# Three more block-product pairs in place of six dense gates, with the page scores moved beside the attention heads

## The chip, the cores and the metric

The kernel runs on one core of a Trainium2 chip. Five engines with queues of their own do the work: PE (TensorE, matrix products, with its weight loads shown as PEld), DVE (VectorE), ACT (ScalarE), POOL (GpSimd) and SP (SyncE, which here only issues transfers). POOL issues transfers too, and all gathers. The metric is the device time of one execution in microseconds (us); lower is better. Cited line numbers, such as L220, are lines of the kernel before.

## The reference

One step of one decoder layer, in float32, for a prompt of 512 tokens and 8 further sequences with one new token each. The kernel puts both side by side as 520 columns (`N`). Cut to what matters:

```python
h = modulate(rmsnorm(x, norm1_w), sh1, sc1)      # shift/scale from a conditioning product with w_ada
mq, mk, mv, mo, mi, mf, fq, fk, fv, ff, ga, gb = split(h @ w_in + b_in)
y_m = mlstm(mq, mk, mv, mo, mi, mf)              # 4 heads, matrix memory
q_f, k_f = rmsnorm(fq, f_qnorm_w), rmsnorm(fk, f_knorm_w)   # per head, 8 heads of 128
y_f = fox(q_f, k_f, fv, log_sigmoid(ff))         # attention with forgetting; the 8 new tokens
                                                 # also attend to 2 pages of 128 cached keys each
merged = sigmoid(ga) * (y_m @ w_proj_a) + sigmoid(gb) * (y_f @ w_proj_b)
x = x + g1 * (merged @ w_out)
h2 = modulate(rmsnorm(x, norm2_w), sh2, sc2)
x = x + g2 * conv_ffn(h2)                        # width 2 x 5632, causal convolution of width 3
```

`ga` and `gb` are 2048 wide: 16 chunks of 128 rows each. The code calls them first gates (0 to 15) and second gates (16 to 31).

## The kernel before

**Precision and tiling.** Everything is stored feature-major: 128 features on the partitions, 520 tokens along the row. A float32 product is made from three products of rounded parts: weights and inputs are split into a high part (a cast on ACT) and a low part (a subtraction on DVE), and high x high, high x low and low x high are added up. The 520 tokens are two halves of 260 columns.

**Dense chunks.** `dense` (L211) makes one chunk of 128 output rows. For 2048 inputs it has 16 steps of six products, 96 products in all. Weights come 8 steps at a time: `wraw` (L162) loads 512 KB on the SP queue into one of eight `raw` tiles, `wtwo` splits them (ACT cast at L177, DVE subtraction at L178) into two pairs of `wh`/`wl` buffers. After each step one entry of the list `bg` is run, which is how the attention work of an earlier head gets in between the products. Before each 8 steps `due` (L189) may run one step of `pending`: an eighth of a conditioning product (`ada_steps`, L504), which takes four `raw` tiles.

**Pairs.** `Pair` (L260) makes two chunks together. The 2 x 2 blocks (two output chunks by two halves of the inputs, against two halves of the tokens) are combined before and after, so that seven block products do for eight: seven times 24 products of 260 columns, 168 in all. `run_pairs` drives a list of pairs with every DVE, ACT and PE instruction in program order. `GatePair` (L1023) applies the sigmoid and writes to DRAM (`dmg` for first gates, `dsg` for second gates).

**Stages around the change**, in order: the mLSTM heads with two first gates done densely (`NG` is 2: gates are made until `bg` is empty); 16 chunks of `y_m @ w_proj_a`; twelve pairs (first gates 2 to 15 and second gates 0 and 1, with the four pairs of attention values); the attention heads, 16 dense chunks `f_proj` (L1254), a query and a key chunk for each of 8 heads; the second gates 2 to 15, 14 dense chunks `w_gate`; 16 chunks of `y_f @ w_proj_b` (8 steps each); then `w_out`, the feed-forward part and the end.

**Attention work in `bg`.** For each head: `f_norm_q`, `f_norm_k` (each with a reciprocal root by `rsqrt`, L360), `f_forget`, `f_values`, four `f_scores`, four `f_turn`, four `f_attend`, at fixed slots of the chunks that follow. A slot is one step of a dense chunk.

**Page work.** The 8 new tokens attend to gathered pages, in steps that all start after the last head: `s_rows` turns the queries into rows and writes them to DRAM; sixteen times `s_load` (queries broadcast by SP, two gathers of keys by POOL) and `s_scores` (on DVE, two multiplications of 512 columns and two reductions); `s_bias`, `s_softmax`, `s_weights`; 32 `s_gather` of values, eight `s_attend` and four `s_heads`. They lie in the 224 slots of the 14 gates.

**What sets the order.** Outside the pairs a planner fixes each engine's order in advance from its own costs. Weight loads and splits are given the highest priority, the rest goes by the order of the text. Tiles of one tag are handed out in the order of the text, each waiting for a free buffer. On the chip each queue then runs in that order, so a waiting instruction holds all behind it.

Of the kernel before, what the change touches and what calls it, by code (L numbers as in the profile page):

```python
# [63 lines left out]
def tile_hybrid_step(ctx: ExitStack, tc: tile.TileContext, I, O):  # L64
# [116 lines left out]
    def wsplit(src, raw=None):  # L181
        with tc.high_priority():
            return wtwo([raw or wraw(src)], src.shape[1])

    pending = []
    calls = [0, 1, 1]
    bg, slow = [], []
# [171 lines left out]
    def rsqrt(parts, scale, out=None):  # L359

        v, r, t = pt("rv"), out or st("rr"), pt("rt")
        for ps, a, b in parts:
            S.activation(r[:, a:b], ps, AF.Ln, scale=scale, bias=eps)
            V.tensor_scalar(v[:, a:b], ps, scale, EPS, op0=ALU.mult, op1=ALU.add)
        o = slice(parts[0][1], parts[-1][2])
        S.activation(r[:, o], r[:, o], AF.Exp, scale=-0.5)
        V.tensor_tensor(t[:, o], r[:, o], r[:, o], op=ALU.mult)
# [132 lines left out]
    def ada_steps(which):  # L500

        box = []
        col0 = which * DM

        def part(k):
            if k == 0:
                box.append(mm_ps("adp"))
            raw = [[wraw(I["w_ada"][i * P:(i + 1) * P, col0 + e * 1024:col0 + (e + 1) * 1024]) for e in range(2)]
                   for i in (k, k + 1)]
            for i in (k, k + 1):  # L510
                ada_mm(box[0], [(i, raw[i - k][g // 2][:, g % 2 * 512:(g % 2 + 1) * 512], i == 0, i == KC - 1)
                                for g in range(4)], False)
# [448 lines left out]
        for i, (a, b) in enumerate(((w[0], x[0]), (w[0], x[1]), (w[1], x[0]))):  # L961
            T.matmul(ps, a, b, start=(first and i == 0), stop=(last and i == 2))

    def on(f, *a):
        return lambda: f(*a)

    for hh in range(MH):
        H = Head()
        H.i, H.vt, H.hm, H.v, H.o = hh, [], [], [], []
# [48 lines left out]
                G.dma_start(dxf[i + 8 * (n == 4)][:, :N], t[:, :N])  # L1018


    dsg = dram([NG, P, N], "dsg")

    class GatePair(Pair):  # L1023
        def __init__(self, gates, order):
# [75 lines left out]
                self.out(0)  # L1100
                self.__dict__.clear()

    gates = list(range(NG, KC + NG))
    units = [GatePair(gates[2 * i:2 * i + 2], ORDER if i else ORDER1) for i in range(KC // 2)]
    units[2:2] = [ValuePair((2 * i, 2 * i + 1)) for i in range(FH // 2)]


# [58 lines left out]

    qwc = mconst([P, 1], "qwc")
    V.tensor_scalar(qwc, col(C_QN), DK ** -0.5, None, op0=ALU.mult)
    qS = mconst([P, NS, FH], "qS")
    kS = mconst([P, NS, FH], "kS")  # L1170
    vS = mconst([P, NS, FH], "vS")
    yf = []

# [4 lines left out]
    def f_norm_k(H):  # L1178
        f_norm(H.k, col(C_KN), H)
        G.dma_start(O["kT"][:, H.i, :], H.k[:, :N])  # L1180
        V.tensor_copy(kS[:, :, H.i], H.k[:, SEQ:N])
        H.kr = split(sp, "s", H.k, "fk", SEQ, G)

    def f_norm_q(H):
        if H.i == 0:
            log_exp()
        f_norm(H.q, qwc, H)
        V.tensor_copy(qS[:, :, H.i], H.q[:, SEQ:N])
        H.qr = split(sp, "s", H.q, "fq", SEQ, G)

    def f_square(H, t):
# [38 lines left out]
    def f_turn(H, j):  # L1230

        w = SEQ - j * P
        ps = mm_ps("fPT")
        for i in range(j, NB):
            T.transpose(ps[:, (i - j) * P:(i - j + 1) * P], H.p[i][:, j * P:(j + 1) * P], ident)
        if j == NB - 1:
            S.copy(H.last[:, P:2 * P], ps[:, :P])
            H.p = None
        else:
            H.pt.append(split(sp, "s", ps, "fp", w))  # L1240

    def f_attend(H, j):
        if j == 0:
            H.y = mm_ps("fy")
        o = slice(j * P, (j + 1) * P)
        if j < NB - 1:
            three(H.y[:, j * P:], [t[:, o] for t in H.vt], [t[:, :SEQ - j * P] for t in H.pt[j]], j == 0, False)
            H.pt[j] = None
# [14 lines left out]
    def slots(at):  # L1263
        bg.extend(at.get(i) for i in range(KC))

    heads = []
    for hh in range(FH + 1):
        if hh < FH:
            H = Head()
            H.i, H.p, H.pt = hh, [], []  # L1270
            H.v = st("fi")
            nc.sync.dma_start(H.v[:, :N], dv[hh])
            heads.append(H)
        A = heads[hh - 1] if hh > 0 else None
        first_half, second_half = {}, {}
        if A:
            first_half = {4: on(f_norm_k, A), 6: on(f_forget, A), 8: on(f_values, A),
                          14: on(f_scores, A, 0), 15: on(f_scores, A, 1)}
            second_half = {0: on(f_scores, A, 2), 2: on(f_scores, A, 3)}
            second_half.update({7 + j: on(f_turn, A, j) for j in range(NB)})  # L1280
            second_half.update({12 + j: on(f_attend, A, j) for j in range(NB)})
        if hh < FH:
            second_half[5] = on(f_norm_q, H)
        slots(first_half)
        if hh == FH:
            bg.extend(second_half.get(i) for i in range(KC))
            break
        H.q = f_proj(H, 0)
        f_square(H, H.q)
        slots(second_half)  # L1290
        H.k = f_proj(H, 1)
        f_square(H, H.k)


    dqf = dram([NS, FH * P], "dqf")
    sc = mconst([P, NPG, NS, FH], "sc")
    pp = st("pp")
    yS = mconst([P, NS, FH], "yS")

    def s_rows():  # L1300
        ps = mm_ps("qSt")
        T.transpose(ps[:64, :P], qS.rearrange("p b h -> p (b h)"), ident)
        qrow = pt("qrow")
        V.tensor_copy(qrow[:64, :P], ps[:64, :P])
        nc.sync.dma_start(dqf.rearrange("b (h d) -> (b h) d", h=FH), qrow[:64, :P])

    def s_load(i):

        b, e = divmod(i, 2)
        qb = pt("qb")  # L1310
        nc.sync.dma_start(qb[:, :512], dqf[b, e * 512:(e + 1) * 512].partition_broadcast(P))
        W.k[i] = [qb]
        for g in range(NPG):
            kp = pt("kp")
            gather(kp[:, :512], I["cache_k"], idx_h[e][:, b * NPG + g:b * NPG + g + 1])
            W.k[i].append(kp)

    def s_scores(i):
        b, e = divmod(i, 2)
        qb, *kps = W.k.pop(i)  # L1320
        v = Ordered(tc, nc.vector)
        for g, kp in enumerate(kps):
            v.tensor_tensor(kp[:, :512], kp[:, :512], qb[:, :512], op=ALU.mult)
            v.tensor_reduce(sc[:, g, b, e * 4:e * 4 + 4], kp[:, :512].rearrange("p (h d) -> p h d", h=4),
                            axis=AX.X, op=ALU.add)

    def s_bias():
        V.tensor_tensor(sc, sc, sbias, op=ALU.add)

    def s_softmax():  # L1330
        pqk = pt("pqk")[:, :64]
        V.tensor_tensor(pqk, qS.rearrange("p b h -> p (b h)"), kS.rearrange("p b h -> p (b h)"), op=ALU.mult)
# [24 lines left out]
    def s_gather(i):  # L1357

        e, g, b = i // 8 % 2, i // 4 % 2, i // 16 * 4 + i % 4
        W.v[i] = pt("vp")  # L1360
        gather(W.v[i][:, :512], I["cache_v"], idx_h[e][:, b * NPG + g:b * NPG + g + 1])

    def s_attend(n):
# [23 lines left out]
    bg += [s_rows] + [None] * 12 + [on(s_load, 0), None, None, on(s_load, 1)] + [None] * 5  # L1387
    for i in range(NS * 2):
        bg += [on(s_scores, i), None] + ([on(s_load, i + 2)] if i + 2 < NS * 2 else []) + [None] * 2
    bg += [s_bias, None, s_softmax] + [None] * 6 + [s_weights] + [None] * 4  # L1390
    bg += [on(s_gather, i) for i in range(6)] + [None] * 4
    for n in range(8):
        bg += [on(s_attend, n)] + [on(s_gather, i) for i in range(n * 4 + 6, min(n * 4 + 10, 32))]
        bg += [on(s_heads, n // 2)] if n % 2 else [None]
        bg += [None] * 3
    mg = []
    for j in range(KC):
        if j == 0:
            assert not pending
            pending += ada_steps(SH2)  # L1400
            calls[:] = 0, 1, 4
        if j < NG:
            mg.append(st("sgm"))
            nc.sync.dma_start(mg[j][:, :N], dsg[j])
        else:
            mg.append(w_gate(j, 1))
    flush()
    for hh in range(FH):
        hi, lo = yf[hh]
        S.copy(hi[:, SEQ:N], yS[:, :, hh])  # L1410
# [144 lines left out]
    for n, j in enumerate(order):  # L1555
# [642 lines left out]
```

## Time and profile before

| | us |
|---|---|
| median of 3 runs | 2924.07 |
| lowest, highest | 2920.72, 2925.45 |
| profiled execution | 2922.52 |
| its span | 2920.8 |
| PE busy in it | 2859.3 |

The profile is of one execution. "Busy" is the time in which at least one instruction of an engine ran. A group of instructions stands with its line, engine and operation, what it writes and reads, its count and the mean of one. Matmuls overlap, so that the mean of one (about 283 ns) is longer than the step from one to the next. The chain of waits says which engine waited for which; the windows give busy times of a stretch of the span.

The stages named above lie at these times of the span: pairs 564 to 809 us, attention heads 809 to 1063, second gates 1063 to 1265, `w_proj_b` 1265 to 1359.

### The profile page before, as it was taken

How to read it: one execution, taken by the hardware profiler on the slowest of the kernel's cores; microseconds unless marked ns; L12 is line 12 of the kernel's file. 1: busy time of each engine (PE TensorE's matmuls, PEld its weight loads, DVE VectorE, ACT ScalarE, POOL GpSimd, SP SyncE). 2: the span in 40 equal slices, each digit the busy share in tenths (PEclk: the TensorE clock that was granted, in tenths of full speed). 3: DMA queues.
4: the chain of work that ended last, by engine and by line, in shares of the span. 5: the costliest groups of instructions: out<-in, count | busy, mean ns of one | idle time of the engine just before them, and what ended most of it. 6: DMA issues, size and time to landing. Idle time of an engine off the chain costs nothing. (4 is left out here: it accounts for less than half of the span.)

```text
span 2920.8 us, 58505 instructions
## 1 busy us (share of the span) xinstructions
PE 2859.3 (98%) x23531; PEld 2737.8 (94%) x23531; DVE 2172.4 (74%) x3950; ACT 1311.3 (45%) x2244; POOL 433.0 (15%) x686
## 2 busy tenths in 40 slices
PE   6999999999999999999999999999999999999999
PEld 4889998999999898899999999999999999999999
DVE  4777875577856657258888888888888888787787
ACT  3234433355544442234555544444444445544543
POOL 0003430211111124311121000000000001100100
PEclk9999999999999999999999999999999999999999
DMA  9933448845444458766772344444434436746742
GB/s 339 302 115 111 151 124 271 292 149 167 157 163 141 139 184 292 261 212 210 216 244 83 113 145 142 134 140 143 151 126 149 137 127 178 196 157 189 201 161 87
DMA packets 211640, 510.92 MB, mean 175 GB/s; under 512 B 23136, under 2 KB 75728, under 8 KB 211368
## 3 DMA queue, kind: packets, MB, share of 16 engines
q1 hardware_dynamic: 175152, 414.37, 43.9%
q0 software_dynamic: 35776, 92.58, 10.7%
q8 instruction: 184, 3.01, 0.4%
q14 instruction: 88, 0.72, 0.1%
q10 hardware_dynamic: 440, 0.23, 0.0%
HBM read 438.77 MB, written 64.86 MB: 172 GB/s over the span
## 5 line engine op out<-in xcount | busy, mean ns | idle before, releaser
L60 PE MATMUL x<-bf,wh 128*128 128x260 f32 x2624 | 477.4, 283 | 1.0 <-DVE tg L60 0.5
L60 ACT CAST wh<-sw 128x512 fp32r<-128x512 f32 x616 | 353.1, 621 | 246.1 <-PE z L60 87.1
L60 DVE TENSOR_TENSOR wl<-sw,wh 128x512 fp32r<-128x512 f32 x616 | 396.5, 685 | 77.1 <-ACT wh L60 73.9
L60 DVE TENSOR_TENSOR wl<-raw,wh 128x1024 fp32r<-128x1024 f32 (+2 forms) x307 | 326.1, 1072 | 118.2 <-ACT wh L60 111.3
L60 PEld LDWEIGHTS x<-bf,wh 128*128 128x128 f32 x2624 | 403.6, 188 | 1.4 <-DVE tg L60 0.7
L60 ACT CAST wh<-raw 128x1024 fp32r<-128x1024 f32 (+2 forms) x307 | 281.8, 929 | 252.9 <-PE x L60 128.7
L60 PE MATMUL x<-bf,wl 128*128 128x260 f32 x1312 | 369.7, 282 | 0.0
L178 DVE TENSOR_TENSOR wl<-raw,wh 128x1024 fp32r<-128x1024 f32 (+1 forms) x152 | 185.5, 1221 | 202.4 <-ACT wh L177 201.9
L177 ACT CAST wh<-raw 128x1024 fp32r<-128x1024 f32 (+1 forms) x152 | 156.8, 1032 | 357.3 <-PE gate L220 114.2
L60 PEld LDWEIGHTS x<-bf,wl 128*128 128x128 f32 x1312 | 247.1, 188 | 0.0
L60 PE MATMUL y<-bf,wh 128*128 128x260 f32 x1312 | 238.5, 282 | 2.8 <-ACT wh L60 2.3
L60 PEld LDWEIGHTS y<-bf,wh 128*128 128x128 f32 x1312 | 201.1, 188 | 3.2 <-ACT wh L60 2.5
L60 DVE TENSOR_TENSOR sw<-raw,raw 128x512 f32<-128x512 f32 x304 | 195.3, 683 | 0.8 <-DMA tot<-sq 0.8
L60 PE MATMUL x<-ff,wh 128*128 128x260 f32 x1024 | 186.0, 282 | 0.0
L60 PE MATMUL y<-bf,wl 128*128 128x260 f32 x656 | 184.6, 281 | 0.2 <-DVE wl L60 0.2
L60 PEld LDWEIGHTS x<-ff,wh 128*128 128x128 f32 x1024 | 157.7, 188 | 0.0
L60 PE MATMUL x<-ff,wl 128*128 128x260 f32 x512 | 144.6, 282 | 0.0
L60 PE MATMUL fo<-fe,wh 128*128 128x260 f32 x768 | 125.5, 284 | 1.1 <-DVE fo L60 0.9
L60 PEld LDWEIGHTS y<-bf,wl 128*128 128x128 f32 x656 | 123.3, 188 | 0.4 <-DVE wl L60 0.4
L60 PE MATMUL z<-bf,wh 128*128 128x260 f32 x656 | 121.3, 285 | 0.0
L60 PEld LDWEIGHTS z<-bf,wh 128*128 128x128 f32 x656 | 100.7, 188 | 13.4 <-issue 13.4
L220 PE MATMUL fi<-hh,wh 128*128 128x260 f32 x512 | 108.9, 294 | 0.0
(589 smaller groups left out, 7624.7 us busy)
## 6 DMA issues: line engine op xcount, KB each, us to landing
raw<-in_w_fi SPq DMA_DIRECT2D x176, 512.0 KB, 4.2
raw<-in_w_in SPq DMA_DIRECT2D x156, 512.0 KB, 4.8
ar<-in_w_ada SPq DMA_DIRECT2D x192, 256.0 KB, 5.9
raw<-in_w_ada SPq DMA_DIRECT2D x96, 512.0 KB, 4.2
raw<-in_w_fo SPq DMA_DIRECT2D x64, 512.0 KB, 4.1
raw<-in_w_out SPq DMA_DIRECT2D x32, 512.0 KB, 5.3
raw<-in_w_fo SPq DMA_DIRECT2D x32, 384.0 KB, 3.9
dff<-cc POOLq DMA_DIRECT2D x44, 260.0 KB, 4.2
```

The lines of the kernel that those rows point to most:

```text
L60: return lambda *a, **k: self.tc.keep_in_program_order(getattr(self.eng, op)(*a, **k))
L177: S.copy(wh[:, o], t[:, :m])
L178: V.tensor_tensor(wl[:, o], t[:, :m], wh[:, o].bitcast(F32), op=ALU.subtract)
L220: T.matmul(acc[:, z, :HN], a[:, o], b[:, z * HN:(z + 1) * HN], start=(k == 0 and i == 0), stop=(k == K - 1 and i == 2))
```

## The change

- Second gates 2 to 7 are made in three more pairs; `GatePair` now does 22 gates. Eight second gates (8 to 15) stay dense. Gates 0 to 7 are fetched from `dsg` during the `w_proj_b` stage, two chunks ahead (`fetch_gate`).
- The bookkeeping of slots becomes a dictionary `plan` from slot to steps, filled by `at(chunk, slot, step)`, with chunks 0 to 15 the heads and 16 to 23 the eight gates.
- The page scores are split by heads: heads 0 to 3 have their `s_rows` at chunk 7 and their eight loads and scores in chunks 8 to 15, beside the later heads; heads 4 to 7 have them in chunks 16 to 18, five slots apart. Values are gathered from chunk 18 on, eight ahead of the first use, half of them into another tile tag.
- The two gathers of one load go into one `raw` tile (the tag of the weight tiles) instead of two small ones, and one multiplication and one reduction of 1024 columns replace two of 512.
- `rsqrt`: the copy of scaled variance plus eps (two halves) and the square move from DVE to ACT.
- `f_turn` does the last block together with the second one; two `f_scores` share a slot.
- Conditioning steps: the last step of a product is now an entry of its own in `pending`; both products of this part are queued at once and run one in three calls in the heads, one in four in the gates, one in two in `w_proj_b`.

```diff
@@ rsqrt
         for ps, a, b in parts:
             S.activation(r[:, a:b], ps, AF.Ln, scale=scale, bias=eps)
-            V.tensor_scalar(v[:, a:b], ps, scale, EPS, op0=ALU.mult, op1=ALU.add)
+            S.activation(v[:, a:b], ps, AF.Identity, scale=scale, bias=eps)
         o = slice(parts[0][1], parts[-1][2])
         S.activation(r[:, o], r[:, o], AF.Exp, scale=-0.5)
-        V.tensor_tensor(t[:, o], r[:, o], r[:, o], op=ALU.mult)
+        S.activation(t[:, o], r[:, o], AF.Square)
@@ ada_steps
-        return [lambda k=k: part(k) for k in range(0, KC - 2, 2)] + [lambda: (part(KC - 2), bg.append(last))]
+        return [on(part, k) for k in range(0, KC, 2)] + [last]
@@ gates
+    NB2 = 8
-    gates = list(range(NG, KC + NG))
+    gates = list(range(NG, KC + NB2))
@@ f_turn
-        for i in range(j, NB):
-            T.transpose(ps[:, (i - j) * P:(i - j + 1) * P], H.p[i][:, j * P:(j + 1) * P], ident)
...
+        for b, c in ((j, 0),) if j != 1 else ((1, 0), (3, w)):
+            for i in range(b, NB):
+                T.transpose(ps[:, c + (i - b) * P:c + (i - b + 1) * P], H.p[i][:, b * P:(b + 1) * P], ident)
@@ page work
     def s_load(i):
-        b, e = divmod(i, 2)
+        e, b = divmod(i, NS)
         qb = pt("qb")
-        nc.sync.dma_start(qb[:, :512], dqf[b, e * 512:(e + 1) * 512].partition_broadcast(P))
-        W.k[i] = [qb]
+        nc.sync.dma_start(qb[:, :512], dqf[e, b].partition_broadcast(P))
+        kp = raw_tile()
+        W.k[i] = qb, kp
         for g in range(NPG):
-            kp = pt("kp")
-            gather(kp[:, :512], I["cache_k"], idx_h[e][:, b * NPG + g:b * NPG + g + 1])
-            W.k[i].append(kp)
+            gather(kp[:, g * 512:(g + 1) * 512], I["cache_k"], idx_h[e][:, b * NPG + g:b * NPG + g + 1])
     def s_scores(i):
...
-        for g, kp in enumerate(kps):
-            v.tensor_tensor(kp[:, :512], kp[:, :512], qb[:, :512], op=ALU.mult)
-            v.tensor_reduce(sc[:, g, b, e * 4:e * 4 + 4], kp[:, :512].rearrange("p (h d) -> p h d", h=4),
-                            axis=AX.X, op=ALU.add)
+        k2 = kp.rearrange("p (g c) -> p g c", g=NPG)
+        v.tensor_tensor(k2, k2, qb[:, :512].unsqueeze(1).to_broadcast([P, NPG, 512]), op=ALU.mult)
+        v.tensor_reduce(sc[:, :, b, e * 4:e * 4 + 4], kp.rearrange("p (g h d) -> p g h d", g=NPG, h=4),
+                        axis=AX.X, op=ALU.add)
@@ the plan
-    pending += ada_steps(SC2)
-    calls[:] = 0, 1, 4
+    pending += ada_steps(SC2) + ada_steps(SH2)
+    calls[:] = 0, 1, 3
...
+        at(c + 1, 5, f_norm_q, H)
+        at(c + 2, 4, f_norm_k, H)
+        at(c + 2, 6, f_forget, H)
+        at(c + 2, 8, f_values, H)
+        at(c + 2, 14, f_scores, H, 0)
+        at(c + 2, 14, f_scores, H, 1)
+        at(c + 3, 0, f_scores, H, 2)
+        at(c + 3, 2, f_scores, H, 3)
...
+    for e, c in enumerate((7, 15)):
+        at(c, 11, s_rows, e)
+        for i in range(1 + e):
+            at(c + 1, i, s_load, e * 8 + i)
+    for i in range(8):
+        at(8 + i, 11 if i % 2 == 0 else 4, s_scores, i)
+        if i < 7:
+            at(8 + i, 12 if i % 2 == 0 else 6, s_load, i + 1)
+        at(16, 9 + 5 * i, s_scores, 8 + i)
+        if i < 6:
+            at(16, 11 + 5 * i, s_load, 10 + i)
+    for i in range(8):
+        at(18, 8 + i, s_gather, i)
+    at(19, 0, s_bias)
+    at(19, 2, s_softmax)
+    at(19, 9, s_weights)
+    for n in range(8):
+        at(19, 13 + 7 * n, s_attend, n)
...
+    calls[:] = 0, 1, 4
...
+    for j in range(NB2, KC):
+        mg[j] = w_gate(j, 1)
     flush()
+    fetch_gate(0)
+    fetch_gate(1)
+    calls[:] = 0, 1, 2
@@ w_proj_b
+        if n % 2 == 0 and n // 2 + 2 < NB2:
+            fetch_gate(n // 2 + 2)
```

More of the change, by code (lines that the diff above doesn't have):

```diff
@@ L1101, in after @@
                 self.__dict__.clear()
-    gates = list(range(NG, KC + NG))
-    units = [GatePair(gates[2 * i:2 * i + 2], ORDER if i else ORDER1) for i in range(KC // 2)]
+    gates = list(range(NG, KC + NB2))
+    units = [GatePair(gates[2 * i:2 * i + 2], ORDER if i else ORDER1) for i in range(len(gates) // 2)]
     units[2:2] = [ValuePair((2 * i, 2 * i + 1)) for i in range(FH // 2)]
@@ L1258, in f_proj @@
         return t
-    pending += ada_steps(SC2)
-    calls[:] = 0, 1, 4
[L1263 to L1295, printed above, removed]
+    pending += ada_steps(SC2) + ada_steps(SH2)
+    calls[:] = 0, 1, 3
+    dqf = dram([2, NS, 4 * P], "dqf")
     sc = mconst([P, NPG, NS, FH], "sc")
@@ L1396, in tile_hybrid_step, with at @@
[L1396 to L1406, printed above, removed]
+    plan = {}
+    def at(chunk, k, f, *a):
+        plan.setdefault(chunk * KC + k, []).append(on(f, *a))
+    heads = []
+    for hh in range(FH):
+        H = Head()
+        H.i, H.p, H.pt = hh, [], {}
+        heads.append(H)
+        c = 2 * hh
+        at(c + 1, 5, f_norm_q, H)
[6 more added lines that the diff above has]
+        at(c + 3, 2, f_scores, H, 3)
+        for k, j in ((7, 0), (8, 1), (9, 2)):
+            at(c + 3, k, f_turn, H, j)
+        for j in range(NB):
+            at(c + 3, 12 + j, f_attend, H, j)
@@ new lines, in tile_hybrid_step, with run @@
+    at(19, 2, s_softmax)
+    at(19, 9, s_weights)
+    for n in range(8):
+        at(19, 13 + 7 * n, s_attend, n)
+        for i in range(n * 4 + 8, min(n * 4 + 12, 32)):
+            at(19, 13 + 7 * n + 1 + i % 4, s_gather, i)
+        if n % 2:
+            at(19, 13 + 7 * n + 3, s_heads, n // 2)
+    def run(fs):
+        for f in fs:
+            f()
+    assert not bg
+    bg += [on(run, plan[i]) if i in plan else None for i in range(max(plan) + 1)]
+    for H in heads:
+        H.q = f_proj(H, 0)
+        f_square(H, H.q)
+        H.v = st("fi")
+        nc.sync.dma_start(H.v[:, :N], dv[H.i])
+        H.k = f_proj(H, 1)
+        f_square(H, H.k)
```

56 lines of the change are left out of this document (26 added, 30 removed).

## The prediction

> **What bounds the kernel now.** I read the page's busy line first, then the windows by stage, then the chain of waits of PE in the two stages that the change rewrites.
>
> ```profile
> PE 2859.3 (98%) x23531; PEld 2737.8 (94%) x23531; DVE 2172.4 (74%) x3950; ACT 1311.3 (45%) x2244; POOL 433.0 (15%) x686
> ```
>
> ```profile
> 459.40:564.20 104.80, 104.80 (x870) 95.38 (x870) 56.50 (x105) 38.58 (x66) 19.98 (x37) 1.00 0.85 289
> 564.20:809.50 245.30, 243.80 (x2029) 243.01 (x2028) 187.98 (x325) 126.90 (x251) 38.54 (x74) 1.00 0.52 171
> 809.50:1062.60 253.10, 250.87 (x2011) 230.94 (x2011) 157.64 (x341) 119.12 (x232) 45.30 (x41) 1.00 0.45 153
> 1062.60:1264.70 202.10, 197.69 (x1598) 176.46 (x1597) 94.24 (x166) 56.62 (x82) 72.14 (x68) 0.99 0.74 253
> ```
>
> Columns: length, then busy time and count of PE, PEld, DVE, ACT and POOL, the granted clock, the DMA share and GB/s. The stages are the `w_proj_a` chunks, the pairs, the heads and the second gates. PE is busy in all of them: 1.5 us idle in the pairs, 2.2 in the heads, 4.4 in the gates. So fewer products shorten the time directly, and nothing else does unless it makes PE wait. The waits of PE in heads and gates:
>
> ```profile
> PE gate L220 <- DVE wl L178: 2.9, 1, 2.9
> PE ms L395 <- POOL lo L387: 2.2, 7, 0.4
> PE sO L1369 <- DMA vp<-in_cache_v,idx: 1.5, 1, 1.5
> ```
>
> The first is one event, and the timeline shows its cause:
>
> ```profile
> 1149.21 9.29 SPq L1311 DMA_DIRECT2D qb<-dqf  x2
> ...
> 1156.13 0.69 DVE L60 TENSOR_TENSOR kp<-kp,qb 128x512 f32<-128x512 f32 x1 [6.23 <-DMA qb<-dqf]
> ...
> 1158.78 1.21 DVE L178 TENSOR_TENSOR wl<-raw,wh 128x1024 fp32r<-128x1024 f32 x1
> ...
> 1160.05 0.80 PE L220 MATMUL gate<-hh,wl 128*128 128x260 f32 x2 [2.91 <-DVE wl L178]
> ```
>
> DVE stood 6.23 us before a page score whose queries had not landed; the weight split queued behind it, and PE ran dry. The loss is more than the 2.9 us of the wait:
>
> ```profile
> 1134.50:1149.00 14.50, 14.50 (x122) 12.93 (x122) 11.78 (x18) 2.69 (x3) 7.35 (x8) 1.00 0.97 331
> 1149.00:1163.50 14.50, 11.59 (x85) 11.38 (x85) 8.10 (x12) 2.69 (x3) 6.24 (x6) 0.88 0.79 275
> 1160.00:1164.00 4.00, 3.95 (x21) 3.95 (x22) 3.93 (x6) 0.00 (x0) 2.92 (x3) 0.61 0.84 246
> ```
>
> 85 products in place of 122 at 104.80 / 870 = 0.1205 us each are 4.4 us lost: the granted clock is 0.61 after the wait. A stall of PE thus costs about 1.5 times its length (4.4 / 2.9).
>
> **The change part by part.**
>
> *Six gates into three pairs.* A dense gate is 96 products (1536 for 16 gates), a pair 168:
>
> ```profile
> 1618.27 2.88 PE x L60 x24
> L220 PE MATMUL gate<-hh,wh 128*128 128x260 f32 x512 | 106.9, 290 | 0.0
> ```
>
> Removed 6 x 96 = 576, added 3 x 168 = 504, so 72 products less; 24 take 2.88 us, so **-8.64 us**. The added pairs' DVE and ACT work is covered as in the present stage, where DVE is busy 187.98 of 245.30 us. Their outputs go to DRAM by POOL, their return by SP comes two `w_proj_b` chunks ahead. At nothing, then; without that cover a late gate would hold a DVE multiply, not a product, for a chunk.
>
> *Page loads and scores.* The gain is that the present stalls lose their cause:
>
> ```profile
> raw<-in_w_ada SPq DMA_DIRECT2D x60, 512.0 KB, 4.4
> raw<-in_w_in SPq DMA_DIRECT2D x55, 512.0 KB, 6.3
> qb<-dqf SPq DMA_DIRECT2D x16, 256.0 KB, 5.0
> kp<-in_cache_k,idx POOLq DMA_INDIRECT x32, 6.2
> L60 DVE TENSOR_TENSOR kp<-kp,qb 128x512 f32<-128x512 f32 x32 | 21.9, 684 | 8.6 <-DMA qb<-dqf 7.3 <-DMA kp<-in_cache_k,idx 1.2
> L60 DVE TENSOR_REDUCE sc<-kp 128x4 f32<-128x512 f32 x32 | 21.9, 685 | 1.0
> L177 ACT CAST wh<-raw x61: 1044/1049/1058, 808.1 to 1264.8; 128x1024 fp32r<-128x1024 f32 x61
> L178 DVE TENSOR_TENSOR wl<-raw,wh x60: 1214/1224/1268, 809.9 to 1256.4; 128x1024 fp32r<-128x1024 f32 x60
> ```
>
> Today queries and both key tiles share eight small buffers, so a load starts when a score ends, while DMA runs at 0.97. Afterwards only the queries use them, and half of the loads fall where DMA is at 0.45. I take the 4.4 us as gone, and half of the 1.5 us before `sO`, whose values are now gathered eight ahead in two tags: **-4.4 and -0.8** (ends: 0 and -5.9).
>
> The price is in the ring of eight `raw` tiles, handed out in order of the text. In the heads that is harmless: over 16 chunks the ring takes 32 weight tiles, 36 conditioning tiles and eight page tiles, 8 slots of lead or more for each. In gate chunks 16 to 18 eight page tiles come in 40 slots, and at chunk 17 slot 8 four conditioning tiles and a weight tile. That weight tile gets the buffer which the score at chunk 16 slot 14 frees: 10 slots of about 202.10 / 14 / 16 = 0.9 us, less the score (four times 0.685, 2.7 us), leave 6.3 us, plus the conditioning step before it (below, 1.92). It needs landing, cast and split: 6.3 + 1.05 + 1.22 = 8.6 us, or 6.7 us with a landing of 4.4. The weight tile after it waits for a conditioning tile freed at the same slot 8, 8 slots or 7.2 us ahead. So PE stands 0 to 0.4 us at the first and 0 to 1.4 at the second, and more where the score is late behind other DVE work. I take 2.0 us of standing, times 1.5: **+3.0** (ends: 0, and 8.7 if both stand as long as the 2.91 us above).
>
> DVE's work in the heads: per head it takes on two scores, 5.4 us, less two reciprocal roots (below), 3.1, and has room, 21.19 of 31.50 us busy now:
>
> ```profile
> 904.50:936.00 31.50, 31.22 (x251) 28.83 (x252) 21.19 (x47) 15.72 (x31) 4.79 (x6) 1.00 0.42 143
> 1062.60:1077.00 14.40, 14.40 (x122) 14.26 (x121) 10.59 (x22) 7.47 (x12) 4.14 (x4) 1.00 0.34 113
> 1077.00:1091.00 14.00, 14.00 (x115) 11.91 (x114) 7.89 (x22) 8.45 (x17) 3.73 (x4) 1.00 0.69 230
> ```
>
> In chunks 16 and 17 five scores come on top of 10.59 + 7.89: 18.5 - 1.6 + 13.5 = 30.4 of 28.4 us. Splits have the highest priority and go in between, and the last scores end in chunk 18; the attend steps end 14 slots before `w_proj_b`, some 12 us, which cover that.
>
> POOL's sixteen gathers there move in among its splits (POOL is busy 4.79 of the 31.50 us, ACT 15.72); SP takes eight query loads and a write. Behind a gather that waits for its buffer stand POOL's splits and so the root sums, which I count in the next part; behind a query load that waits for the rows stand weight loads, with a chunk of lead.
>
> *Reciprocal root.* Per use two copies of 428 ns and a square of 700 ns leave DVE:
>
> ```profile
> L364 DVE TENSOR_SCALAR rv<-ms x42: 416/428/430, 23.0 to 1069.1; 128x260 f32<-128x260 f32 x42
> L367 DVE TENSOR_TENSOR rt<-rr x21: 699/700/702, 25.4 to 1069.7; 128x520 f32<-128x520 f32 x21
> L60 ACT ACTIVATE fo<-fo,ada 128x260 f32<-128x260 f32 x64 | 26.9, 471 | 5.4 <-PE fo L60 5.4
> L1193 ACT ACTIVATE sq<-fi x16: 637/640/642, 822.9 to 1064.7; 128x520 f32<-128x520 f32 x16
> ```
>
> ACT gets 2 x 0.47 + 0.64 = 1.58 us, DVE loses 1.56. The copies ran beside ACT's exponential, so the chain grows by 0.94 + 0.64 - 0.70 = 0.9 us. In the heads that meets the second score, which also moves one slot earlier:
>
> ```profile
> 944.10 1.31 POOL L232 TENSOR_TENSOR fkl<-fi,fkh 128x512 fp32r<-128x512 f32 x1
> 946.28 0.28 PE L962 MATMUL fS<-fkh,fqh 128*128 128x256 f32 x1
> ```
>
> The low part ends at 945.41, 0.87 us before its use. 0.9 later and 0.7 earlier turn that into -0.7. The planner will put other products first, as it does for the root sums, which still wait 0.3 us each for POOL (the 2.2 us above). Between nothing and 8 x 0.31 = 2.5 I take **+1.0**, gather delays included. Before the feed-forward part the root is used alone:
>
> ```profile
> 1536.32 0.46 ACT L60 ACTIVATE rr<-ms,eps 128x260 f32<-128x260 f32 x1
> ```
>
> A copy as long as this logarithm now stands behind it on ACT; the square only changes its engine: 0 to 0.5, **+0.3**. At the start and in the mLSTM heads other waits (weights, gates) cover it.
>
> *Conditioning steps.* Each costs the same anywhere:
>
> ```profile
> 955.00 1.92 PE L418 MATMUL adp<-raw,cs 128*32 128x512 f32 x16
> ```
>
> One goes from the gates to the heads, two to `w_proj_b`, where one call in two is the rate at which `w_proj_a` runs without a gap (104.80 of 104.80, 289 GB/s): 0. Turning blocks together and splitting `s_rows` move or add one or two transposes: 0.
>
> **Sum.** -8.64 - 4.4 - 0.8 + 3.0 + 1.0 + 0.3 = -9.5 us on the profiled execution's 2922.52, so 2913.0. The median of the runs is 1.55 us above that execution, and the forecast for it is 2924.07 - 9.5 = **2914.5 us**.
>
> **The rivals.**
>
> *The ring takes it back (2920).* The two pinched weight tiles cost their upper end, 8.7 in place of 3.0: -3.8 in all. For it: page tiles are held 8 slots and DVE is full there. Against: PE's waits above hold none for the load of a `raw` tile. 0.15.
>
> *Slower: page tiles starve the weights at every load (2935).* Each of the 16 loads holds one of eight buffers, up to 21 slots in the heads. It decides from 15.4 us on (5.85 for the bound below, plus 9.5), about 1 us per load; 1.3 us of loss each give +20.8 - 9.5 = +11. For it: weights and pages now share buffers. Against: in the heads a weight tile comes only every 8 slots, and landing, cast and split need 8.6 us of the 8 slots x 0.9 that even one free buffer gives. 0.13.
>
> [...]
>
> 0.07.
>
> *All stalls go (2908.5).* No new wait, and the old ones all gone: -8.64 - 5.9 - 1 of the POOL waits = -15.5. 0.15.
>
> **How the numbers follow.** About 0.2% (5.85 us) is what a measurement of this kernel can tell from no change: under 2918.2 is faster, above 2929.9 slower. Forecast 0.50 and all-stalls 0.15 are faster; the ring rival and the POOL rival, 0.22, are within; starving 0.13 is slower. The range 2907 to 2928 takes in all but the starving case and little of the rest: down to no new wait at all, up to the upper ends of ring and scores (8.7 + 2.5) with the old stalls kept; the forecast's own range is 2910 to 2919.
>
> [...]
>
> **What would show it.** The pair stage longer by 3 x 20.2 us and the gates shorter by 6 x 11.5 and more; 23459 or so PE instructions, but for the transposes; no DVE wait for queries of several us; PE waiting for a split near chunk 17 slot 8, by 1 to 3 us. Wrong if PE waits for weight splits in the heads, or if DVE stands before gathered keys.

## The result, and the profile after

The changed kernel takes 2935.58 us (median, 2933.77 to 2936.64), the kernel before 2924.07 us. The ratio is 1.004 with a 95% interval of 1.0026 to 1.0055: **slower by 0.4%**, where 2914.5 us and a gain had been forecast. Its profiled execution has a span of 2932.0 us, 11.2 us more than before.

The page's busy line of the changed kernel:

```profile
PE 2856.4 (97%) x23460; PEld 2730.7 (93%) x23460; DVE 2165.9 (74%) x3915; ACT 1353.1 (46%) x2356; POOL 443.5 (15%) x698
```

There are 71 PE instructions fewer (72 products were priced), and PE is busy for 2.9 us less, while the span is 11.2 us longer. So the time lost is mostly idle time of PE. The windows of the changed kernel by stage (columns as before): the mLSTM stage from 210.30 us on, `w_proj_a`, the pairs, the heads, the second gates and `w_proj_b`.

```profile
210.30:463.00 252.70, 241.37 (x1863) 227.37 (x1862) 182.65 (x328) 112.36 (x178) 80.31 (x84) 1.00 0.42 133
463.00:567.60 104.60, 104.60 (x869) 95.15 (x868) 56.64 (x106) 38.88 (x66) 19.98 (x37) 1.00 0.84 288
567.60:873.20 305.60, 304.10 (x2533) 303.27 (x2532) 233.59 (x399) 158.35 (x314) 45.14 (x86) 1.00 0.49 162
873.20:1144.30 271.10, 258.25 (x2023) 233.32 (x2023) 152.37 (x320) 136.46 (x275) 74.81 (x67) 0.99 0.52 174
1144.30:1273.10 128.80, 124.46 (x978) 106.96 (x977) 53.28 (x99) 41.32 (x68) 44.74 (x42) 0.99 0.72 247
1273.10:1371.70 98.60, 98.60 (x821) 93.88 (x820) 71.03 (x122) 35.74 (x55) 8.29 (x16) 1.00 0.75 250
```

Against before: `w_proj_a` and pairs together +60.2 us (350.0 to 410.2; 3 x 20.2 = 60.6 was priced); heads and gates together -55.3 (455.2 to 399.9); `w_proj_b` +4.0; the mLSTM stage +3.4; all behind it -1.1. Six dense gates (6 x 11.5) and the two conditioning steps that went to `w_proj_b` (2 x 1.92) should have taken 72.9 us out of heads and gates. **17.6 us are missing there**, and 3.4 in the mLSTM stage. PE's waits in heads and gates of the changed kernel, the longest four:

```profile
PE ms L398 <- POOL lo L390: 5.3, 8, 1.8
PE fS L965 <- POOL fkl L235: 5.3, 3, 4.1
PE gate L223 <- ACT wh L177: 3.2, 2, 3.0
PE fPT L1238 <- DVE fs L1227: 2.5, 3, 1.6
```

The old waits for queries and for gathered values are gone. In their place PE waits 10.6 us for POOL, 4.1 of them in one event, and 3.2 us for weight casts, 3.0 in one event. The first event, in the timeline of POOL and PE of the changed kernel (start, duration, instruction, idle time before it):

```profile
1114.32 1.87 POOL L654 DMA_INDIRECT raw<-in_cache_k,idx  x1 [2.49 <-PE adp L421]
1116.50 1.09 POOL L654 DMA_INDIRECT raw<-in_cache_k,idx  x1 [0.31 <-issue]
1117.90 1.23 POOL L654 DMA_INDIRECT raw<-in_cache_k,idx  x1 [0.30 <-issue]
1119.43 0.95 POOL L654 DMA_INDIRECT raw<-in_cache_k,idx  x1 [0.30 <-issue]
1120.68 1.20 POOL L654 DMA_INDIRECT raw<-in_cache_k,idx  x1 [0.30 <-issue]
1122.18 0.95 POOL L654 DMA_INDIRECT raw<-in_cache_k,idx  x1 [0.31 <-issue]
1123.13 0.59 POOL L1182 DMA_DIRECT2D out_kT<-fi  x1
1123.75 1.28 POOL L235 TENSOR_TENSOR fkl<-fi,fkh 128x512 fp32r<-128x512 f32 x1
...
1125.08 0.58 PE L965 MATMUL fS<-fkl,fqh 128*128 128x256 f32 x1 [4.12 <-POOL fkl L235]
```

Six gathers of keys stand in POOL's queue ahead of the low part `fkl`. The first waits for a `raw` tile that a conditioning step (`adp`) still reads, then each holds POOL for 0.95 to 1.87 us. PE stands for 4.12 us. The second event has ACT's cast of a weight tile late, because the tile itself landed late:

```profile
1177.10 1.04 ACT L177 CAST wh<-raw 128x1024 fp32r<-128x1024 f32 x1 [2.55 <-DMA raw<-in_w_in]
...
1178.20 0.80 PE L223 MATMUL gate<-hh,wh 128*128 128x260 f32 x2 [3.00 <-ACT wh L177]
```

This is the ring's pinch of the forecast, at the place that it named. 144 gate products stand before the first product that waits for a weight cast there (0.20 us, at 1174.16): the 96 of chunk 16 and 48 of chunk 17, which is slot 8. Four products later PE stands the 3.00 us for the next weight tile. The timeline of DVE, SP and PE shows what the loads of these two tiles had waited for:

```profile
1167.43 1.20 DVE L60 TENSOR_REDUCE sc<-raw 128x8 f32<-128x1024 f32 x1
1168.66 0.33 SPq L163 DMA_DIRECT2D raw<-in_w_in  x1
...
1170.46 1.06 PE L421 MATMUL adp<-raw,cs 128*32 128x512 f32 x6
1171.54 0.33 SPq L163 DMA_DIRECT2D raw<-in_w_in  x1
```

The first load starts 0.03 us after a page score has ended, the second 0.02 us after a conditioning step has. What both events cost, in windows of the changed kernel around them:

```profile
1113.00:1129.00 16.00, 11.88 (x83) 10.14 (x84) 8.09 (x12) 5.91 (x11) 9.15 (x8) 0.83 0.74 242
1174.00:1184.00 10.00, 6.84 (x42) 6.58 (x43) 7.55 (x8) 1.59 (x4) 8.05 (x7) 0.83 0.97 356
```

At 0.1205 us a product 16 us hold 133 and 10 us hold 83. So 50 products, 6.0 us, and 41 products, 4.9 us, were lost, about 1.5 and 1.6 times the waits. This is an estimate, since attention products of other lengths stand among them. Together it is 10.9 of the 17.6 us that are missing in heads and gates.

In the mLSTM stage PE has waits that before had none of (waits of PE, changed kernel):

```profile
PE ST L801 <- DVE nmb L781: 4.6, 3, 1.5
```

### The profile page after: what moved, and what is told of

Same layout as the page of the kernel before. It is cut to its first block, busy times and chain, and to the rows that moved or that the text cites. A ratio compares the mean times of both kernels' runs of the same rounds, so it can differ in the third digit from the quotient of the medians.

```text
span 2932.0 us, 58501 instructions
## 1 busy us (share of the span) xinstructions
PE 2856.4 (97%) x23460; PEld 2730.7 (93%) x23460; DVE 2165.9 (74%) x3915; ACT 1353.1 (46%) x2356; POOL 443.5 (15%) x698
## 3 DMA queue, kind: packets, MB, share of 16 engines
q0 software_dynamic: 36352, 94.18, 10.6%
## 5 line engine op out<-in xcount | busy, mean ns | idle before, releaser
L60 ACT CAST wh<-sw 128x512 fp32r<-128x512 f32 x640 | 366.8, 621 | 245.1 <-PE z L60 88.8
L60 DVE TENSOR_TENSOR wl<-sw,wh 128x512 fp32r<-128x512 f32 x640 | 412.7, 687 | 82.6 <-ACT wh L60 79.7
L60 DVE TENSOR_TENSOR wl<-raw,wh 128x1024 fp32r<-128x1024 f32 (+2 forms) x325 | 337.9, 1052 | 119.7 <-ACT wh L60 114.5
L60 ACT CAST wh<-raw 128x1024 fp32r<-128x1024 f32 (+2 forms) x325 | 292.2, 913 | 267.1 <-PE x L60 126.1
L178 DVE TENSOR_TENSOR wl<-raw,wh 128x1024 fp32r<-128x1024 f32 (+1 forms) x140 | 172.5, 1233 | 218.0 <-ACT wh L177 217.3
L177 ACT CAST wh<-raw 128x1024 fp32r<-128x1024 f32 (+1 forms) x140 | 144.1, 1030 | 277.5 <-PE gate L223 59.6
L60 DVE TENSOR_TENSOR sw<-raw,raw 128x512 f32<-128x512 f32 x316 | 203.3, 685 | 0.8 <-DMA tot<-sq 0.8
L60 PE MATMUL x<-hf,wh 128*128 128x260 f32 x720 | 131.7, 283 | 1.0 <-ACT wh L60 0.6
```

The source lines that it names most:

```text
L60: return lambda *a, **k: self.tc.keep_in_program_order(getattr(self.eng, op)(*a, **k))
L177: S.copy(wh[:, o], t[:, :m])
L178: V.tensor_tensor(wl[:, o], t[:, :m], wh[:, o].bitcast(F32), op=ALU.subtract)
```

## The experiments

Three theories were set against each other: **Q**, the gathers in POOL's queue hold the heads' low parts; **R**, the longer chain of the root delays its readers; **W**, page tiles in the ring of `raw` tiles take the weights' buffers. The expectations name them so.

All times by stage stand in one table, worked out from the windows of each kernel as above (us, of one profiled execution each; "root", "keys" and "low parts" say on which engine or in which tiles; the last two columns are the ratio to the kernel before and its interval). The kernel before was timed again beside each group of runs, with medians of 2919.63 to 2924.07 us, so kernels of different groups are best compared by the ratios.

| kernel | root | keys | low parts | mLSTM | heads | gates | ratio | 95% |
|---|---|---|---|---|---|---|---|---|
| before | DVE | small | POOL | 249.3 | 253.1 | 202.1 | 1 | |
| after | ACT | ring | POOL | 252.7 | 271.1 | 128.8 | 1.0040 | 1.0026 to 1.0055 |
| e1 | ACT | ring, pinned | POOL | 255.3 | 289.6 | 136.8 | 1.0146 | 1.0133 to 1.0160 |
| e2 | ACT | ring | DVE | 254.4 | 262.8 | 134.6 | 1.0044 | 1.0030 to 1.0057 |
| e3 | DVE | ring | POOL | 250.6 | 266.0 | 133.0 | 1.0039 | 1.0025 to 1.0052 |
| e4 | ACT | small | POOL | 252.7 | 265.1 | 126.4 | 1.0024 | 1.0014 to 1.0033 |
| f1 (before + root) | ACT | small | POOL | 255.2 | 255.0 | 200.2 | 1.0028 | 1.0017 to 1.0039 |
| f2 (before, no keys) | DVE | none | POOL | 248.9 | 253.3 | 196.3 | 0.9990 | 0.9981 to 0.9999 |
| f3 (after, no keys) | ACT | none | POOL | 252.7 | 259.7 | 119.7 | 0.9988 | 0.9978 to 0.9997 |
| f4 | DVE | small | POOL | 247.1 | 261.5 | 132.7 | 1.0014 | 1.0005 to 1.0023 |
| g1 (after, no keys) | DVE | none | POOL | 248.8 | 257.2 | 119.7 | 0.9958 | 0.9944 to 0.9971 |
| g2 (softmax later) | DVE | small | POOL | 249.9 | 261.0 | 130.3 | 1.0012 | 1.0003 to 1.0021 |
| g3 (softmax later) | DVE | small | DVE | 249.6 | 256.9 | 127.0 | 0.9979 | 0.9970 to 0.9988 |
| g4 (softmax later) | DVE, ACT from the heads on | small | POOL | 249.6 | 264.7 | 122.7 | 0.9994 | 0.9985 to 1.0003 |
| h1 (softmax later) | DVE | ring | DVE | 247.8 | 259.5 | 130.4 | 1.0012 | 1.0003 to 1.0021 |

### One cause taken away from the changed kernel at a time

*e1: the key gathers keep their place in the text, behind the splits that stand before them.*

```diff
-            gather(kp[:, g * 512:(g + 1) * 512], I["cache_k"], ...)
+            tc.keep_in_program_order(gather(kp[:, g * 512:(g + 1) * 512], I["cache_k"], ...))
```

> The changed kernel with one edit: each gather of page keys is kept in program order on POOL's queue, so that it stands behind the split that was written before it, not ahead of it. Theory Q (POOL's queue: gathers ahead of the splits keep PE waiting for the split parts): PE's waits for POOL in heads and gates fall from 10.6 us to about 2 us, and with the clock loss of 1.5 times the kernel gets about 12 us faster, to about 2923. Rival R (the roots' longer chain on ACT makes the splits late): the order on POOL does not matter, 2935. Rival W (page tiles take the weights' buffers): pinned gathers hold the ring longer, PE waits more for weight splits, 2935 or more.

Measured 2962.81 us, ratio 1.0146. PE's waits for `fkl` fall to 0.8 us, but in heads and gates it now waits 14.0 us at `fy` for the probabilities' parts and 8.5 us for weight casts and splits. The pin changed the planner's order on more than POOL's queue, so this run doesn't tell Q from W; it shows only that this order is worse.

*e2: the heads' low parts go to DVE.*

```diff
-        H.kr = split(sp, "s", H.k, "fk", SEQ, G)
+        H.kr = split(sp, "s", H.k, "fk", SEQ, V)     # H.qr and parts_r(sq) alike
```

> The changed kernel with the low parts of keys, queries and squares in the attention heads made on DVE; POOL keeps only gathers and stores. Theory Q: no wait of PE for POOL in heads and gates (10.6 us today), some 14 to 16 us faster, about 2920, less what DVE's 2.8 us more per head cost. Rival R: the chain in front of the splits is as long as before, PE waits as long, only for DVE: 2933. Rival W: the waits for weight casts (3.2 us) stay; 2931.

Measured 2933.83 us, ratio 1.0044: no gain. The waits for POOL are gone and the heads are 8.3 us shorter, but the gates are 5.8 us longer, with 3.7 us of waiting for weight casts and a clock of 0.97. Q was there, as the heads show, but its 2920 us did not come: the waits for weight casts, which W names, stood behind it.

*e3: the root as before.*

```diff
-            S.activation(v[:, a:b], ps, AF.Identity, scale=scale, bias=eps)
+            V.tensor_scalar(v[:, a:b], ps, scale, EPS, op0=ALU.mult, op1=ALU.add)
...
-        S.activation(t[:, o], r[:, o], AF.Square)
+        V.tensor_tensor(t[:, o], r[:, o], r[:, o], op=ALU.mult)
```

> The changed kernel with the two copies and the square of the reciprocal root back on DVE. In the mLSTM heads PE's new wait before the scores (4.6 us in three waits) goes, about 3.5 us. Theory Q: the waits for POOL in heads and gates stay at about 10 us: 2932. Rival R: they go with the 0.9 us shorter chain: about 2920.

Measured 2932.53 us, ratio 1.0039. The mLSTM stage is shorter by 2.1 us, its waits at `ST` are gone, and the heads are shorter by 5.1, with 6.4 us of waiting for POOL in place of 10.6; the gates take 4.2 back, with 4.9 us of waiting for weight casts.

*e4: each page's keys in a small tile of their own, as before the change; the ring is left to weights and conditioning.*

```diff
-        kp = raw_tile()
+            kp = pt("kp")                # one for each page
```

> The changed kernel with page keys again in two small tiles of the other tag and two scores of 512 columns; the ring of weight tiles holds weights only. Rival W: PE's wait for weight casts (3.2 us, one of 3.0) goes, and with it the gathers' waits for weight splits: about 2922. Theory Q: what counts is where gathers stand on POOL's queue; six in a row are no longer possible with eight small tiles, so the longest wait (4.1 us) goes, about 6 us with the clock loss, while shorter ones stay: about 2928. Rival R: 2935.

Measured 2928.04 us, ratio 1.0024: the largest gain of the four, heads and gates 8.4 us shorter together, and no wait for a weight cast in the gates. But 6.0 of the 8.4 us are in the heads, where PE's waits for `fkl` fall from 5.3 to 1.1 us, and the time is the 2928 that Q gave, not W's 2922. This run takes away the six gathers in a row and the pinch of the ring at once, so it doesn't tell them apart; and the kernel stays slower than before.

### One part alone, and the keys taken out

*f1: the kernel before with the root of the change* (the diff of e3, reversed).

> The kernel before with one part of the change alone: the copies of the root and its square on ScalarE. Theory R (the longer root chain moves the mLSTM stage's order, so that the score products there wait for the decay bias): the mLSTM stage is 3 to 4 us longer, with three waits of PE at line 798 of about 1.5 us, and the whole is 3 to 5 us slower than before (ratio 1.001 to 1.0017). Rival, as forecast: 0.3 to 1.3 us, within what can be told from no change.

Measured 2929.14 us, ratio 1.0028, which is 8.2 us, above both expectations: in its profiled execution +5.9 us in the mLSTM stage, +1.9 in the heads, -1.9 in the gates and +1.7 behind them. How the root got there is seen in the mLSTM stage. The timeline of ACT, DVE and PE in the kernel before, around the first of the three places:

```profile
286.30 0.84 ACT L363 ACTIVATE rr<-ms,eps 128x260 f32<-128x260 f32 x2 [1.70 <-PE ms L395]
287.17 1.28 ACT L366 ACT_TABLE_LOAD   x1
288.46 0.64 ACT L366 ACTIVATE rr<-rr 128x520 f32<-128x520 f32 x1
...
291.21 0.69 DVE L368 SCALAR_TENSOR_TENSOR rt<-rt,rv 128x520 f32<-128x520 f32 x1
...
296.64 0.68 DVE L778 COPY nmb<-nMb 128x512 f32<-128x512 f32 x1
...
297.38 0.49 PE L798 MATMUL ST<-pre,pre 128*128 128x128 f32 x2
```

And in f1:

```profile
287.39 0.48 ACT L363 ACTIVATE rr<-ms,eps 128x260 f32<-128x260 f32 x1
289.03 1.05 ACT L177 CAST wh<-raw 128x1024 fp32r<-128x1024 f32 x1 [1.16 <-PE mv L220]
289.99 0.47 ACT L364 ACTIVATE rv<-ms,eps 128x260 f32<-128x260 f32 x1
290.47 1.28 ACT L366 ACT_TABLE_LOAD   x1
291.77 0.64 ACT L366 ACTIVATE rr<-rr 128x520 f32<-128x520 f32 x1
...
293.11 0.70 DVE L368 SCALAR_TENSOR_TENSOR rt<-rt,rv 128x520 f32<-128x520 f32 x1 [1.45 <-ACT rt L367]
...
298.54 0.68 DVE L778 COPY nmb<-nMb 128x512 f32<-128x512 f32 x1
...
299.28 0.49 PE L798 MATMUL ST<-pre,pre 128*128 128x128 f32 x2 [1.55 <-DVE nmb L778]
```

Before, the decay bias `nmb` ended at 297.32 us and PE's product began at 297.38: a margin of 0.06 us. In f1 the second copy stands on ACT behind a weight cast that itself waits 1.16 us for PE, and the exponential with its table load stands behind the copy: it starts at 291.77 in place of 288.46, of which 0.36 us were there before the first logarithm. DVE's next step and `nmb` are 1.9 us late, and PE waits 1.55 us; there are three such waits in the stage, 4.6 us together. The table load takes 1.28 us in both kernels; in f1 it starts 0.01 us after the copy's end, and the exponential 0.02 us after the load's. The table of stages shows the same for every profiled execution: 252.7 to 255.3 us in this stage with the root on ACT, 247.1 to 250.6 with it on DVE.

*f2, f3, g1: without page keys.* The edit is the same in both kernels; g1 has the root as before as well.

```diff
     def s_load(i):
+        return
...
     def s_scores(i):
+        if i == 0: V.memset(sc, 0.0)
+        return
```

> The kernel before without page keys: the loads of queries and keys and the page scores are left out, the scores are zeros. Both theories: the stall for late queries goes and with it 4.4 us or somewhat more, so 5 to 8 us faster than before. It is the base for the next one.

> The changed kernel without page keys, loads and scores left out in the same way. Theory K (the page keys' place, in the ring and in POOL's queue, eats the gain; the pairs themselves save what was priced): against the kernel before without page keys -8.6 of the pairs and +3 to +4 of the roots, so 4 to 6 us faster than that one, and some 10 to 13 us faster than before. Rival U (pairs, or the written order of the heads, cost time by themselves): no faster than the kernel before without page keys.

> The changed kernel without page keys (loads and scores of the keys are left out, zeros in their place) and with the root as before, so that of the change only the pairs, the placed steps and the conditioning steps are left. Theory S (the saving of the pairs arrives, the root costs what its run alone showed): 8 to 9 us faster than the kernel before without page keys, ratio to before about 0.996, and no wait of PE for the decay bias in the mLSTM stage. Rival (the pairs or the written order take back a part): within 4 us of the kernel before without page keys, ratio 0.998 or more.

Measured 2916.96, 2917.04 and 2908.50 us. f2 is only 3.4 us faster than before, not 5 to 8. Heads and gates of g1, in its windows:

```profile
869.50:1126.70 257.20, 254.80 (x2033) 232.47 (x2033) 154.80 (x351) 119.58 (x231) 45.32 (x41) 1.00 0.48 159
1126.70:1246.40 119.70, 119.39 (x969) 103.95 (x968) 36.13 (x82) 40.38 (x65) 35.53 (x36) 1.00 0.63 212
```

Together 376.9 us, which is 72.7 less than f2's 449.6, where 72.9 were priced; g1 is 8.5 us faster than f2. The pairs give what they were to give. With the root on ACT all of it is gone: f3 is as fast as f2, not the 4 to 6 us faster that theory K forecast, and not 10 to 13 us faster than before.

This gives one split of the change, by medians and with some 4 us of uncertainty: the pairs -8.5 (g1 to f2); the root +8.5 (f3 to g1; 8.2 in f1); the page keys cost 3.4 us before (before to f2, 2920.37 beside it) and 15.0 after (1.0040 x 2920.37 = 2932.0, less 2917.04), +11.6. Together +11.6; measured +11.5. That these add up is no proof, since each difference starts where another ends and the measured whole is in them. What is measured twice is the price of the pairs (8.64 forecast, 8.5 measured) and that of the root with no ring behind it (8.2 and 8.5).

The split also depends on the order. In the changed kernel with its ring, the root back on DVE gains 0.3 us by the ratios (after to e3), and taking the keys out behind it gains 24 (e3 to g1). With small tiles the root is worth 2.9 us (e4 to f4). The causes don't add: what one leaves free, another takes.

### What the page keys' 15 us consist of, and a version that beats both

*f4: keys in small tiles and the root as before* (e4 and e3 together).

> The changed kernel with the keys in two small tiles each, so that the ring serves weights alone, and with the root as before. If the two causes stand apart, the gains add: about 3 us less than with small tiles alone, ratio to before about 1.001. If the roots on DVE cost the heads what they give the mLSTM stage, ratio 1.002 to 1.003 as with small tiles alone.

Measured 2923.83 us, ratio 1.0014. The mLSTM stage gains 5.6 us and the heads 3.6, but the gates lose 6.3: PE stands 5.3 us before the turned scores (`sS`). *g2: the same with the softmax later.*

```diff
-    at(19, 0, s_bias)
-    at(19, 2, s_softmax)
-    at(19, 9, s_weights)
+    at(19, 5, s_bias)
+    at(19, 7, s_softmax)
+    at(19, 13, s_weights)                # the attend steps four slots later
```

> Keys in small tiles, root as before, and the page softmax and all behind it five slots later. If the 5.3 us for which PE stood before the scores' transposes is what was left of the page keys' cost, that wait goes, the gates take 126 to 127 us in place of 132.7, and the whole is 1 to 3 us faster than before (ratio 0.999 to 1.0). If the scores only arrive later still, or the attend steps hold the stage behind, the ratio stays at 1.001 or above.

Measured 2924.72 us, ratio 1.0012. The wait only falls to 4.3 us (PE's waits in g2):

```profile
PE sS L1304 <- DVE sc L1297: 4.3, 1, 4.3
PE ms L398 <- POOL lo L390: 3.8, 8, 1.0
```

A later slot didn't put the product later: the bias on the scores ends 59.0 us after the first gate's first product in f4 and 58.3 in g2, and PE waits for it in both. With the root on ACT in the heads it ends 50.6 us (e4) and 51.1 us (g4) after that product; PE's wait is 1.9 us in e4, and g4 has none. About half of that is only the longer heads: counted from the start of the heads it ends 3.5 to 4.9 us earlier. That DVE has less work there is the likely reason, which no run takes apart.

*g3: as g2, with the low parts on DVE* (the diff of e2). *g4: as g2, with the root on DVE up to the mLSTM stage's end and on ACT from the heads on.*

> The same with the heads' low parts on DVE in place of POOL. If POOL's queue (gathers ahead of splits) still costs the heads, the waits for POOL (3.8 us) go and the heads are 3 to 5 us shorter than 261.5. If DVE is the tighter engine, as where the low parts alone were moved, the scores end later still and the gates give it back: no faster than the kernel with the low parts on POOL.

> Keys in small tiles, softmax five slots later, root on DVE up to the mLSTM stage's end and on ScalarE from the heads on. If the root's cost is that of the mLSTM stage alone, this one is as fast as the one with the root on DVE throughout, or faster, since DVE has less in the heads. If the longer chain costs the heads too, heads are 3 to 4 us longer (265 us as against 261.5).

g3 takes 2916.12 us, ratio 0.9979 (0.9970 to 0.9988): **faster than before and than the change**. Its heads take 256.9 us; taking four low parts per head out of POOL's queue gives 8.6 us, the same edit that gave nothing in e2. Not all of this is the gathers' doing: PE's waits for POOL in g2 are 4.0 us, and 1.9 us of such waits stand in the kernel without keys too (g1). g4 takes 2918.78 us, ratio 0.9994: its gates are the shortest of all kernels with the keys, 122.7 us, but its heads are 3.7 us longer than g2's. The longer root chain costs the heads too (2.5 us between f3 and g1).

*h1: as g3, but with the keys in the ring.*

> As the kernel with small tiles, the root as before, the softmax five slots later and the low parts on DVE (ratio 0.9979), but with the keys in the ring of raw tiles as in the change. What differs is the ring alone, with root and POOL's splits out of its way. If the ring takes weights' buffers, PE waits for ACT's casts in the gates as it did with the low parts alone on DVE (3.7 us, clock 0.97), and it is 4 to 8 us slower than with small tiles: ratio 0.9995 to 1.0005. If the ring cost something only through the gathers ahead of POOL's splits, it is as fast as with small tiles, ratio 0.998.

Measured 2922.18 us, ratio 1.0012, above the expected 0.9995 to 1.0005. Keys in the ring cost 6 us by the medians and 10 by the ratios. One thing goes with the ring: the score is one multiplication and one reduction of 1024 columns in place of two of 512. Windows of the first gates in h1:

```profile
1145.00:1160.00 15.00, 11.91 (x84) 8.48 (x82) 11.65 (x28) 7.16 (x14) 5.68 (x6) 1.00 0.60 181
1160.00:1170.00 10.00, 7.82 (x46) 7.50 (x45) 7.51 (x8) 1.58 (x3) 7.40 (x7) 0.66 1.02 396
```

PE's two waits there, in the timeline of h1:

```profile
1158.71 0.51 PE L223 MATMUL gate<-hh,wh 128*128 128x260 f32 x2 [3.09 <-ACT wh L177]
1162.51 0.80 PE L223 MATMUL gate<-hh,wh 128*128 128x260 f32 x2 [2.18 <-ACT wh L177]
```

The same windows of g3:

```profile
1145.00:1160.00 15.00, 15.00 (x123) 12.89 (x122) 13.13 (x35) 9.33 (x18) 4.99 (x6) 1.00 0.82 274
1160.00:1170.00 10.00, 10.00 (x82) 9.87 (x81) 9.75 (x17) 4.62 (x8) 5.82 (x6) 1.00 0.90 324
```

130 products in place of 205 are 9.0 us lost to two waits of 5.3 us together. (g3 waits 3.1 us for the scores further on, h1 doesn't, which leaves 3.4 us between their gates; another 2.6 us are in the heads.) Again 144 gate products stand before the first wait and 148 before the second, as in e2, e3 and the changed kernel: the two pinched weight tiles of the forecast, at chunk 17 slot 8.

## Why the prediction was wrong

Two terms of the sum failed. By the split above the root costs 8.5 us, where the sum had 1.3, gather delays included; and the keys' move costs 11.6 us, where it had -2.2 (-4.4, -0.8 and +3.0). Term by term:

- **Six gates into pairs, -8.64:** right. -8.5 between g1 and f2, and the stages agree within 0.4 us.
- **The old stalls, -4.4 and -0.8:** the waits are gone, as said. But the keys' new place brought more than it took away: 15.0 us for 3.4.
- **Reciprocal root, "at the start and in the mLSTM heads other waits (weights, gates) cover it":** this is the first step that failed. Nothing covered it: it was put at nothing and measured 4.6 us of waiting, because PE's product had 0.06 us of margin behind a chain that the root stands in. The stage is 3.4 us longer in the changed kernel and 5.9 in f1. The error was to price copies and square by their own durations (0.47 and 0.64 us) and to count no queue on ACT: the copy fell behind a weight cast, and the exponential behind the copy. The stage held the answer in its trace, and the prediction didn't look there.
- **The heads, +1.0 for root and gathers together:** the second step that failed. It was sized from one wait of 0.31 us. The root costs the heads 1.9 us (f1), 2.5 (f3 to g1), 3.6 (e4 to f4), 3.7 (g4 to g2) or 5.1 (after to e3), to which no single wait was found. The gathers ahead of POOL's low parts cost 6.0 us in one event, and taking the low parts off POOL shortens the heads by 8.3 us (after to e2). The text had named the place, POOL's splits behind a gather that waits for its buffer, and gave it no price of its own. It had called the ring harmless in the heads. For weights it is, but the first of the six gathers waited for a conditioning tile.
- **Feed-forward part, +0.3:** right. From the start of the quoted logarithm to the end of DVE's last step it is 2.29 us before and 2.52 after.
- **The ring near chunk 17, +3.0 (0 to 8.7):** the mechanism and the place were right, to the slot, and the size was too small. It cost 4.9 us in the changed kernel and 9.0 us in h1, just above the upper end. The forecast gave the second tile 8 slots of lead; in the traces PE comes to it after four products of the first, and stands 3.00 us there in the changed kernel and 2.18 in h1, in place of 0 to 1.4 (at the first tile 0.20 and 3.09, in place of 0 to 0.4).
- **A stall costs 1.5 times its length:** right in size for the new ones as well, an estimate each: 6.0 us for 4.12, 4.9 for 3.00, and 9.0 for 5.3 in h1.
- **Conditioning steps at nothing, pairs' cover at nothing:** right; `w_proj_b` is 4.0 us longer for two steps and has no gap.
- **The rivals:** the slower one had page tiles starving weights at every load in the heads. The time it gave, 2935, came true, its mechanism didn't: in the heads PE waits for no weight split. The waits came at two places, and not from the ring alone. That the time fits is luck. Neither sign of being wrong was seen: PE waits for no weight split in the heads, and DVE doesn't stand before gathered keys. The signs looked at neither the root nor POOL.
- **Why removing one cause gave so little:** e2 and e3 shortened the heads by 8.3 and 5.1 us, and the gates took 5.8 and 4.2 of it back, where the waits for weight casts grew from 3.2 us to 3.7 and 4.9. That an earlier stall had hidden a part of the ring's pinch fits this; no run shows it by itself. The ring's waits are longest with the other two away (h1, 5.3 us).

Left open: where the root's time in the heads goes in detail; the 2 us or so of its 8.5 that lie outside the mLSTM stage and the heads (3.9 and 2.5 us between f3 and g1); and what the pin of e1 moved.

## What to carry to other kernels

Before an operation is moved to another engine, look at every place where it is used for the margin between the end of the chain that it stands in and the product that reads it, and put the operation behind what stands in the new engine's queue there; its own duration says little (with copies of 0.47 us and a square of 0.64 us on ACT, `nmb` came 1.9 us late in f1). A transfer that may wait for its buffer should not share a queue with work that a tight chain needs (PE stood 4.12 us for `fkl` behind six gathers in the changed kernel), and buffers that feed the bottleneck should not be lent to others (PE stood 5.3 us for weight casts in h1). When several causes hide one another, taking away one alone may show next to nothing; take the suspected work out altogether and put the parts back one by one, and don't take the prices found in one order for those of another.

## What the runs showed of the hardware

Each of the six gathers of 128 rows of 512 numbers ahead of `fkl` in the changed kernel holds POOL's queue for 0.95 to 1.87 us, with 0.3 us between two, about as long as the subtraction of 512 columns behind them (1.28 us); the prediction had given gathers the time to landing and none on their queue. The granted clock was 0.83 in each of the two windows of the changed kernel around PE's gaps of 4.12 and 3.00 us; in h1 it was 1.00 in the window with the gap of 3.09 us and 0.66 in the next one, with that of 2.18.
